# A hybrid decoder layer on one core: the output projection in seven block products instead of eight

## The chip, the cores and the metric

The kernel runs on one core of a Trainium2 chip. The metric is the device time of one execution in microseconds (us); the value given for a kernel is the median of its runs. The core has a matrix engine (TensorE, PE in the profile), three elementwise engines (VectorE = DVE, ScalarE = ACT, GpSimd = POOL), and SyncE (SP), which here only starts transfers. Each engine works through its own queue strictly in order and waits at the head of it for whatever its next instruction needs.

## The reference

One layer for x of 512 tokens by 1024 channels, all in float32. Two token mixers (a retention with 8 heads and a gated delta rule with 8 heads) are merged by sigmoid gates; their merged output is multiplied by `w_o` (1024 x 1024) and added to x; a gated MLP with a short causal convolution follows. What matters here:

```python
merged = jax.nn.sigmoid(gate_r) * y_ret + jax.nn.sigmoid(gate_d) * y_dn
h = h + merged @ w_o[l]

u2 = rmsnorm(h, g_ffn[l])
up = causal_dwconv(u2 @ w_up[l], ffn_conv_w[l]) + ffn_conv_b[l]
a, b = jnp.split(up, 2, axis=-1)
h = h + (jax.nn.silu(a) * b) @ w_down[l]
```

## The kernel before

**Products.** A float32 operand is split into two fp32r parts, hi (a cast) and lo (the value minus hi), and a product is made of three matmuls: hi by hi, lo by hi, hi by lo. All matmuls are issued from line 175 and all transposes from line 179, so groups are told apart by tile: `pvt`, `pqk`, `pm`, `psc` belong to the two mixers, `pz` and `py` to the gates and branch projections, `po` is the output projection, `pa` and `pb` the up projection, `pd` the down projection. Every elementwise operation goes through one helper, line 160.

**Weights.** They come as blocks of 128 x 1024 numbers: SP loads a block into one of 4 `wraw` tiles (lines 242 and 244), ACT casts it to `whi`, DVE subtracts to get `wlo` (`weights()`; 4 tiles of each). A block that has been used frees its tiles for the block four places later.

**Seven products.** The four matrices of the gates and branches (`matrix(s)`, s = 0 to 3, tile `py`) and the down projection are multiplied as 2 x 2 blocks with seven products of blocks instead of eight (table `PRODUCTS`). Four of the seven need sums of weight blocks (`SUMS`), which POOL makes beforehand in memory by transfers that copy or accumulate, 1 MB each (`presum`, line 265). They are paced: `presums(which, parts, (start, end, n))` sends a piece when the order's clock passes its time, and each piece is preceded by a one-column copy on ACT (`tick`) and one on POOL that waits for it (`tock`).

**The output projection before.** `dense_r` makes it plainly: 8 weight blocks, 192 matmuls of 128 x 512 on all four token tiles. Its operand is made by `m_out`: four transposes on PE (`pmt`), a cast on ACT (`mh`), a subtraction on DVE (`ml`). `o_done` adds each result to `h1`, which is loaded from x (line 1262) after the last branch matrix; then come the sum of squares (`junk`, `ssq`), its root (`rs` on DVE, `rr` on POOL), the scaling (`hs`, two instructions a token tile), four transposes (`pt`), and the split into `u2hi` (ACT) and `u2lo` (DVE), 8 each a token tile. The first three up-projection blocks are made in two halves of 256 tokens (`dense_c_halves`), so that they can start when two of the four token tiles are ready.

**The order.** The program is written in the order in which a small planner, `Order`, takes its steps: `spawn` adds a step with a delay, `poll` lets steps run that are due by the planner's clock, `hold` runs them until an operand exists. The order on PE, DVE, ACT and POOL stays as written. So a change of one time in the planner moves rows on all engines.

Of the kernel before, what the change touches and what calls it, by code (L numbers as in the profile page):

```python
# [18 lines left out]
P = 128  # L19
T = 512  # L20
# [36 lines left out]
DOWN = 4  # L57
INNER = (HK, HK, HK, HK, NK)
# [5 lines left out]
def quarter_blocks(s):  # L64
    n = INNER[s]
    return [("q", s, name, i, min(2, n - 2 * i)) for name, _ in PRODUCTS for i in range((n + 1) // 2)]


def weight_blocks():
# [14 lines left out]
    for o in (0, 512):  # L84
        b += [("r", "w_o", 2 * i, o) for i in range(4)]
# [96 lines left out]
def body(nc, tc, ctx, io):  # L182
# [66 lines left out]
    sums = {(s, n): dram.tile([P, 512 * INNER[s] + 64], F32, name=f"{n}_{s}") for s in range(5) for n, _, _ in SUMS}  # L249
# [84 lines left out]
    def dense_c_halves(x, names, ready_half, first=None):  # L334

        ws, pss = [], [PS(n) for n in names]
        for hf in range(2):
            c = ck(hf, 256)
            for i, ps in enumerate(pss):
                if hf == 0:  # L340
                    ws.append(take("c"))
# [6 lines left out]
                if hf:  # L348
                    used()
# [33 lines left out]
    def product(p, opnd, nk, accs, tail=0):  # L383
# [7 lines left out]
        def block(i, t, c, ps, first):  # L391
# [136 lines left out]
    def fetch_more():  # L528
        free[0] += RAWB - 2
# [171 lines left out]
    spawn(presums(range(3), 1, (90.0, 325.0, 24)), 30.0)  # L701
# [475 lines left out]
    spawn(presums((3,), 1, (order.clock + 5.0, order.clock + 75.0, 8)))  # L1177
    mh, ml = {}, {}
# [3 lines left out]
    def m_tile(k, t):  # L1182
        i = k // HK
        if (t, i) not in ml:
            return None
        return mh[t, i][:, ck(k % HK)], ml[t, i][:, ck(k % HK)]

    def m_out(t, i, r):
# [3 lines left out]
        hi, lo = S(f"mh{t}{i}", F32R), S(f"ml{t}{i}", F32R)  # L1192
        yield from split(hi, lo, pt)
        mh[t, i], ml[t, i] = hi, lo
# [22 lines left out]
    def matrix(s, opnd):  # L1217
# [17 lines left out]
        def prod(p, accs, tail=0):  # L1235
            now[0] = len(PRODUCTS) * s + p
            product(p, opnd, HK, accs, tail)
# [21 lines left out]
    h1 = [[S(f"h1_{t}{i}") for i in range(2)] for t in range(NT)]  # L1259
    for t in range(NT):  # L1260
        for i in range(2):
            sp.dma_start(h1[t][i], xv[t, :, ck(i, T)])
# [4 lines left out]
    def o_done(i):  # L1267
        def done(t, _, ps):
            vec.tensor_tensor(h1[t][i], ps, h1[t][i], ALU.add)
            yield  # L1270
            junk = S("junk")
            half_ssq(ssqs[t], i, h1[t][i], junk)
            if i == 0:
                return
            yield
            rr = s4("rr", 1)
            yield from row_scale(ssqs[t], rr)
            yield
            for i2 in range(2):
                xs = S("hs")  # L1280
                vec.tensor_scalar(xs, h1[t][i2], rr, None, ALU.mult)
                spawn(u2_out(t, i2, xs), 0.6 * (i2 + 1))
        return done
# [14 lines left out]
    for i in range(2):  # L1298
        dense_r([PS("po") for _ in range(NT)], m_tile, done=o_done(i), groups=((0, 1), (2, 3)) if i else ((2, 3), (0, 1)))
# [56 lines left out]
    pss = dense_c_halves(u2, ("pa", "pb", "pa"), u2_half)  # L1356
# [66 lines left out]
    def down(p, accs, tail=0):  # L1423
        at[0] = p
        product(p, parts, NK, accs, tail)
# [101 lines left out]
```

## Time and profile before

| | us |
|---|---|
| median of 3 runs | 1020.42 |
| the runs | 1019.91 to 1023.36 |
| the profiled execution's own time | 1017.77 |
| its span, first to last instruction | 1016.1 |
| PE busy | 992.6 |
| DVE busy | 716.9 |
| ACT busy | 514.9 |
| POOL busy | 154.7 |

The profile comes from one execution, so durations and places are read against 1017.77 us, and a difference found there is then carried to the median. Times in rows count from the start of the span. A row of the timeline gives start, duration, engine, line, operation, output and inputs, count, and in brackets how long the engine stood idle before it and what released it. Matmuls overlap: a row says 0.39 us for a matmul, but in a full pipe the next starts 0.227 us later. Likewise the next instruction of DVE can start a little before the row of the one ahead ends.

### The profile page before, as it was taken

What the parts mean: (1) busy time and instruction counts of PE and PEld (TensorE: products, weight loads), DVE (VectorE), ACT (ScalarE), POOL (GpSimd) and SP (SyncE); (2) the same over time, 40 slices, a digit from 0 to 9 for tenths busy, and PEclk for the clock granted to TensorE, in tenths of its full rate; (3) what the DMA queues carried; (4) which work ended last, traced back from release to release, by engine and by line L of the source; (5) the groups of instructions that cost most, each with busy time, mean ns of one, the idle gap of its engine ahead of it and who ended that gap; (6) DMA issues with size and microseconds to landing.
All of it is one profiled execution on the core that took longest, in us unless ns stands there. A gap on an engine that the chain in (4) does not pass through costs nothing.

```text
span 1016.1 us, 14340 instructions
## 1 busy us (share of the span) xinstructions
PE 992.6 (98%) x5265; PEld 827.2 (81%) x5265; DVE 716.9 (71%) x1344; ACT 514.9 (51%) x1092; POOL 154.7 (15%) x204
## 2 busy tenths in 40 slices
PE   7999899999999999999999998999999999999997
PEld 7888788787788887878888886898888888888886
DVE  4867699456777797647688984576555666778785
ACT  4699312276445423547676652454344343356664
POOL 3021311123222211211110000211121121000001
PEclk8999999999999999999999999999999999999999
DMA  7253659736846853027998656556589988336663
GB/s 242 84 152 107 186 167 209 197 121 159 173 162 177 196 130 109 27 77 270 281 302 244 189 193 212 178 192 212 191 170 197 199 178 189 99 120 190 204 191 120
DMA packets 78550, 177.75 MB, mean 175 GB/s; under 512 B 22864, under 2 KB 31376, under 8 KB 78480
## 3 DMA queue, kind: packets, MB, share of 16 engines
q1 hardware_dynamic: 54160, 120.22, 36.1%
q0 software_dynamic: 24320, 56.63, 25.5%
q8 instruction: 41, 0.67, 0.3%
q14 instruction: 29, 0.24, 0.1%
HBM read 173.64 MB, written 59.80 MB: 230 GB/s over the span
## 4 chain that ended last, share of the span: by engine, by line
PE 76%; DVE 13%; DMA 4%; issue 2%; ACT 2%; POOL 1%; SPq 1%; POOLq 0%; DVEq 0%; ACTq 0%
PE py L175 14%; PE pb L175 12%; PE pa L175 12%; PE pd L175 10%; PE po L175 4%; PE pq L175 4%; PE pk L175 3%; PE pz L175 3%; PE pv L175 3%; DVE wlo L160 3%; DVE xtmp L160 3%; PE psc L175 2%; DVE xx L160 2%; PE pm L175 1%; PE pr L175 1%
## 5 line engine op out<-in xcount | busy, mean ns | idle before, releaser
L160 ACT CAST whi<-wraw 128x1024 fp32r<-128x1024 f32 x206 | 213.4, 1036 | 153.0 <-PE py L175 41.4
L160 DVE TENSOR_TENSOR wlo<-wraw,whi 128x1024 fp32r<-128x1024 f32 x206 | 248.4, 1206 | 45.9 <-ACT whi L160 45.4
L160 POOL TENSOR_SCALAR tock<-tick 128x1 f32<-128x1 f32 x64 | 21.0, 328 | 466.0 <-ACT tick L160 466.0
L160 DVE SCALAR_TENSOR_TENSOR acc<-pb,prm,acc 128x511 f32<-128x511 f32 (+1 forms) x44 | 33.0, 749 | 57.2 <-ACT acc L160 56.4
L175 PE MATMUL pa<-u2lo,whi 128*128 128x512 f32 (+1 forms) x192 | 71.5, 372 | 0.1
L175 PE MATMUL pa<-u2hi,whi 128*128 128x512 f32 (+1 forms) x192 | 71.4, 372 | 0.0
L175 PE MATMUL pa<-u2hi,wlo 128*128 128x512 f32 (+1 forms) x192 | 71.4, 372 | 0.0
L175 PE MATMUL pb<-u2hi,whi 128*128 128x512 f32 (+1 forms) x184 | 70.0, 380 | 0.0
L175 PE MATMUL pb<-u2lo,whi 128*128 128x512 f32 (+1 forms) x184 | 70.0, 380 | 0.0
L175 PE MATMUL pb<-u2hi,wlo 128*128 128x512 f32 (+1 forms) x184 | 70.0, 380 | 0.0
L175 PE MATMUL py<-whi,oh 128*128 128x512 f32 x160 | 62.7, 392 | 0.0
L175 PE MATMUL py<-wlo,oh 128*128 128x512 f32 x160 | 62.4, 390 | 0.0
L175 PE MATMUL py<-whi,ol 128*128 128x512 f32 x160 | 62.3, 390 | 0.0
L175 PE MATMUL pd<-whi,T 128*128 128x512 f32 (+1 forms) x198 | 55.4, 366 | 0.0
L175 PE MATMUL pr<-whi,uhi 128*128 128x512 f32 x128 | 53.0, 414 | 0.0
L175 PE MATMUL pz<-uhi,whi 128*128 128x512 f32 x128 | 52.3, 409 | 0.0
L175 PE MATMUL pr<-whi,ulo 128*128 128x512 f32 x128 | 50.6, 395 | 0.0
L175 PE MATMUL pr<-wlo,uhi 128*128 128x512 f32 x128 | 50.5, 394 | 0.0
L175 PE MATMUL pz<-uhi,wlo 128*128 128x512 f32 x128 | 50.0, 391 | 0.0
L175 PE MATMUL pz<-ulo,whi 128*128 128x512 f32 x128 | 50.0, 390 | 0.0
L160 DVE SCALAR_TENSOR_TENSOR acc<-pa,prm,acc 128x511 f32<-128x511 f32 (+1 forms) x44 | 33.0, 749 | 19.0 <-ACT acc L160 18.2
L175 PEld LDWEIGHTS pa<-u2lo,whi 128*128 128x128 f32 x192 | 36.2, 188 | 6.6 <-DVE u2lo L160 0.3
(313 smaller groups left out, 2447.6 us busy)
## 6 DMA issues: line engine op xcount, KB each, us to landing
wraw<-w SPq DMA_DIRECT2D x108, 512.0 KB, 4.3
wraw<-s SPq DMA_DIRECT2D x52, 512.0 KB, 4.4
s<-wm POOLq DMA_DIRECT2D x24, 1024.0 KB, 6.9
s<-wd POOLq DMA_DIRECT2D x24, 704.0 KB, 5.5
wraw<-wm SPq DMA_DIRECT2D x24, 512.0 KB, 5.8
s<-s POOLq DMA_DIRECT2D x8, 1024.0 KB, 10.9
wraw<-wd SPq DMA_DIRECT2D x15, 512.0 KB, 3.6
s<-s POOLq DMA_DIRECT2D x8, 704.0 KB, 8.9
```

The lines of the kernel that those rows point to most:

```text
L160: return f(out, *args, **kw)
L175: self.engine.matmul(out, lhsT, rhs, start=start, stop=stop, **kw)
```

## The change

The output projection becomes an instance of the seven products, as matrix `OUT` = 4 (the down projection becomes 5). It is 168 matmuls on 14 weight blocks instead of 192 on 8. The products come in the order 0, 3, 2, 5, 4, 1, 6, that is with the operands B11, T1, T2, B22, T3, B21, T4 of the merged activations. `m_out` now copies the transposed tile to memory (`mr`, ACT), DVE makes the combinations T1 to T4 (`mt1` to `mt4`), and each operand is split (cast on ACT, subtraction on DVE, tiles `mB11`, `mT1` and so on). `o_into` adds 14 results to `h1` instead of 8. The token tiles 2 and 3 are complete before 0 and 1, so the first up-projection halves are made in the order second, first.

Times that go with it: the weight sums of matrices 0 to 2 start at 110 of the planner's clock instead of 90 (end and count as before); those of matrix 3 start within the stage of the z gates instead of after it; those of `w_o`, 8 pieces, run from the end of matrix 0; the 8 loads of `h1` move from behind matrix 3 to ahead of it. `fetch_more` waits for a condition; the rows on SP at that place read as before.

```diff
-DOWN = 4
-INNER = (HK, HK, HK, HK, NK)
+OUT, DOWN = 4, 5
+INNER = (HK, HK, HK, HK, HK, NK)
+OUT_ORDER = (0, 3, 2, 5, 4, 1, 6)
...
-    spawn(presums(range(3), 1, (90.0, 325.0, 24)), 30.0)
+    spawn(presums(range(3), 1, (110.0, 325.0, 24)), 30.0)
...
         if x == "d":
             spawn(u_raw(), 8.0)
+            spawn(presums((3,), 1, (order.clock + 8.0, order.clock + 70.0, 8)))
...
-    spawn(presums((3,), 1, (order.clock + 5.0, order.clock + 75.0, 8)))
...
+        m = o_raw[name, half] = S(f"mr{t}{i}")
+        act.copy(m, pt)
+        yield
+        if name in ("B11", "B21"):
+            spawn(o_split(name, half, m))
+        if name == "B12":
+            t1 = S("mt1")
+            vec.tensor_tensor(t1, o_raw["B11", half], m, ALU.subtract)
+            spawn(o_split("T1", half, t1), 0.2)
+            yield
+            t3 = S("mt3")
+            vec.tensor_tensor(t3, o_raw["B22", half], m, ALU.subtract)
+            t2 = o_raw["T2", half] = S("mt2")
+            vec.scalar_tensor_tensor(t2, t3, -1.0, o_raw["B11", half], ALU.mult, ALU.subtract)
+            spawn(o_split("T2", half, t2), 0.2)
+            yield 1.5
+            spawn(o_split("B22", half, o_raw["B22", half]), 0.2)
+            spawn(o_split("T3", half, t3), 1.8)
+        elif name == "B21":
+            yield 1.5
+            t4 = S("mt4")
+            vec.scalar_tensor_tensor(t4, o_raw["T2", half], -1.0, m, ALU.mult, ALU.subtract)
+            spawn(o_split("T4", half, t4), 0.2)
...
+    spawn(presums((OUT,), 1, (order.clock, order.clock + 75.0, 8)))
+    h1 = [[None] * 2 for _ in range(NT)]
     for s, opnd in ((1, u_opnd), (2, d_opnd), (3, r_opnd)):
+        if s == 3:
+            for t in range(NT):
+                for i in range(2):
+                    h1[t][i] = S(f"h1_{t}{i}")
+                    sp.dma_start(h1[t][i], xv[t, :, ck(i, T)])
         matrix(s, opnd)
...
-    for i in range(2):
-        dense_r([PS("po") for _ in range(NT)], m_tile, done=o_done(i), groups=((0, 1), (2, 3)) if i else ((2, 3), (0, 1)))
+    A, E, C = ([PS("po") for _ in range(2)] for _ in range(3))
+    product(0, o_get, HK, [[(full, A[t], True, o_into(t, 0, A[t], ALU.add))] for t in range(2)])
+    product(3, o_get, HK, [[(full, E[t], True, o_into(2 + t, 1, E[t], ALU.subtract))] for t in range(2)])
+    product(2, o_get, HK, [[(full, A[t], False, o_into(2 + t, 0, A[t], ALU.add))] for t in range(2)])
+    product(5, o_get, HK, [[(full, E[t], False, o_into(2 + t, 0, E[t], ALU.add, True))] for t in range(2)])
+    product(4, o_get, HK, [[(full, A[t], False, o_into(2 + t, 1, A[t], ALU.subtract, True))] for t in range(2)])
+    product(1, o_get, HK, [[(full, C[t], True, o_into(t, 0, C[t], ALU.add, True))] for t in range(2)])
+    product(6, o_get, HK, [[(full, A[t], False, o_into(t, 1, A[t], ALU.subtract, True))] for t in range(2)], tail=2)
...
-    pss = dense_c_halves(u2, ("pa", "pb", "pa"), u2_half)
+    pss = dense_c_halves(u2, ("pa", "pb", "pa"), u2_half, order_=(1, 0))
```

Where the change moves rows, three places matter for the prediction. (In these rows the lines of the changed kernel are one higher, since it has one line more at its head.)

POOL, before, in the first heads of the delta rule. `ssk` and `ssqq` are sums of squares of the keys and queries of a head, `rk` and `rq` their roots, `gb` the head's decay tile, `s` a weight sum in memory:

```order
L160 TENSOR_TENSOR rq<-ssqq,mhalf 128x4
L160 TENSOR_SCALAR tock<-tick 128x1
L265 DMA s_0_77<-wm 128x4x512
L160 TENSOR_TENSOR rk<-ssk,mhalf 128x4
L160 AFFINE_SELECT gb_967<-gb_967 128x512
L160 MEMSET xx 64x1024
```

POOL at the same place now:

```order
L161 TENSOR_TENSOR rq<-ssqq,mhalf 128x4
L161 TENSOR_TENSOR rk<-ssk,mhalf 128x4
L161 AFFINE_SELECT gb_971<-gb_971 128x512
L161 MEMSET xx 64x1024
L161 MEMSET xx 64x32
L161 TENSOR_TENSOR rq<-ssqq,mhalf 128x4
L161 TENSOR_SCALAR tock<-tick 128x1
L266 DMA s_0_77<-wm 128x4x512
```

The first `tock` and its transfer stood ahead of the fourth head's `rk`; they now stand behind everything that this head asks of POOL.

DVE, before, at the beginning of the output projection (numbers tell tiles apart; `ml20` is the lo part of token tile 2, first half of the channels):

```order
L160 TENSOR_TENSOR wlo_6260<-wraw_6134,whi_6247 128x1024
L160 TENSOR_TENSOR ml20_6253<-pmt_6197,mh20_6252 128x512
L160 TENSOR_TENSOR ml30_6263<-pmt_6255,mh30_6262 128x512
L160 TENSOR_TENSOR ml01_6276<-pmt_6266,mh01_6275 128x512
L160 TENSOR_TENSOR ml11_6301<-pmt_6290,mh11_6300 128x512
L160 TENSOR_TENSOR h1_20_6206<-po_6240,h1_20_6206 128x512
```

DVE now, from the second half's T3 to the lo part of T2 (`mT2_6395`) that product 2 reads; further on, nine rows later, stands the lo part of B22 (`mB22_6471`) that product 5 reads:

```order
L161 TENSOR_TENSOR mt3_6384<-mr31_6216,mr30_6314 128x512
L161 SCALAR_TENSOR_TENSOR mt2_6386<-mt3_6384,mr10_6096 128x512
L161 TENSOR_TENSOR h1_00_5878<-h1_00_5878,po_6295 128x512
L161 TENSOR_TENSOR h1_10_5882<-h1_10_5882,po_6296 128x512
L161 TENSOR_TENSOR mT4_6382<-mt4_6376,mT4_6381 128x512
L161 SCALAR_TENSOR_TENSOR mt4_6416<-mt2_6386,mr11_6378 128x512
L161 TENSOR_TENSOR wlo_6418<-wraw_6253,whi_6391 128x1024
L161 TENSOR_TENSOR mT2_6395<-mt2_6386,mT2_6394 128x512
```

Before, DVE had four subtractions there; now combinations, splits and additions follow one another.

DVE, before, where the first two token tiles are scaled, in the middle of the output projection:

```order
L160 SCALAR_TENSOR_TENSOR rs_6525<-ssq1_6235 128x1
L160 TENSOR_SCALAR hs_6550<-h1_10_6204,rr_6524 128x512
L160 TENSOR_SCALAR hs_6552<-h1_11_6205,rr_6524 128x512
L160 TENSOR_TENSOR wlo_6558<-wraw_6386,whi_6535 128x1024
L160 SCALAR_TENSOR_TENSOR u2lo0_6226<-pt_6527,prm_99,u2hi0_6218 128x128
```

DVE now, at its end. `h1_11` is the last addition, which needs the last matmul of product 6:

```order
L161 TENSOR_TENSOR h1_11_5884<-h1_11_5884,po_6296 128x512
L161 TENSOR_TENSOR wlo_6688<-wraw_6629,whi_6672 128x1024
L161 SCALAR_TENSOR_TENSOR rs_6693<-ssq1_6294 128x1
L161 TENSOR_TENSOR wlo_6695<-wraw_6653,whi_6685 128x1024
L161 SCALAR_TENSOR_TENSOR junk_6699,ssq1_6291<-h1_01_5880 128x512
L161 TENSOR_SCALAR hs_6702<-h1_20_5886,rr_6679 128x512
L161 TENSOR_SCALAR hs_6704<-h1_21_5888,rr_6679 128x512
L161 SCALAR_TENSOR_TENSOR junk_6706,ssq1_6292<-h1_11_5884 128x512
L161 TENSOR_SCALAR hs_6725<-h1_30_5890,rr_6692 128x512
L161 TENSOR_SCALAR hs_6727<-h1_31_5892,rr_6692 128x512
L161 SCALAR_TENSOR_TENSOR u2lo0_6283<-pt_6708,prm_103,u2hi0_6275 128x128
```

The scaling of the first two finished token tiles, which stood in the middle of the projection with po matmuls after it, now stands behind its last addition; on PE the 16 transposes `pt` of these tiles stand behind the last po matmul.

More of the change, by code (lines that the diff above doesn't have):

```diff
@@ L65, in quarter_blocks @@
     n = INNER[s]
-    return [("q", s, name, i, min(2, n - 2 * i)) for name, _ in PRODUCTS for i in range((n + 1) // 2)]
+    order = OUT_ORDER if s == OUT else range(len(PRODUCTS))
+    return [("q", s, PRODUCTS[p][0], i, min(2, n - 2 * i)) for p in order for i in range((n + 1) // 2)]
 def weight_blocks():
@@ L246, in fetch @@
             raws[i] = raw
-    sums = {(s, n): dram.tile([P, 512 * INNER[s] + 64], F32, name=f"{n}_{s}") for s in range(5) for n, _, _ in SUMS}
+    sums = {(s, n): dram.tile([P, 512 * INNER[s] + 64], F32, name=f"{n}_{s}") for s in range(DOWN + 1) for n, _, _ in SUMS}
     def quarter(s, name):
@@ L416, in product, with by_half, get @@
                 spawn(then, 0.1 if tail else 0.1 + 0.7 * t)
+    def by_half(x):
+        def get(name, k, t):
+            return (name, k) in x and tuple(a[:, ck(t)] for a in x[name, k])
+        return get
     def halves(a):
@@ L528, in fetch_more @@
     def fetch_more():
+        while "G" not in have:
+            yield 0.5
         free[0] += RAWB - 2
@@ L1176, in body, with o_get, o_split @@
     spawn(all_operands())
-    spawn(presums((3,), 1, (order.clock + 5.0, order.clock + 75.0, 8)))
-    mh, ml = {}, {}
     gates = [{}, {}]
     merged = {}
[L1182 to L1186, printed above, removed]
+    o_raw, o_opnd = {}, {}
+    def o_get(name, k, t):
+        return (name, t) in o_opnd and tuple(a[:, ck(k)] for a in o_opnd[name, t])
+    def o_split(name, t, src):
+        hi, lo = S(f"m{name}", F32R), S(f"m{name}", F32R)
+        yield from split(hi, lo, src)
+        o_opnd[name, t] = hi, lo
     def m_out(t, i, r):
@@ L1191, in m_out @@
         yield
-        hi, lo = S(f"mh{t}{i}", F32R), S(f"ml{t}{i}", F32R)
-        yield from split(hi, lo, pt)
-        mh[t, i], ml[t, i] = hi, lo
+        name, half = f"B{i + 1}{t // 2 + 1}", t % 2
+        m = o_raw[name, half] = S(f"mr{t}{i}")
[21 more added lines that the diff above has]
+            spawn(o_split("T4", half, t4), 0.2)
     def gate_end(s, t, i, r, ps):
@@ L1236, in prod @@
             now[0] = len(PRODUCTS) * s + p
-            product(p, opnd, HK, accs, tail)
+            product(p, by_half(opnd), HK, accs, tail)
         A, C = ([PS("py") for _ in range(2)] for _ in range(2))
@@ L1265, in body, with o_into @@
     ssqs = [s4("ssq1", 2) for _ in range(NT)]
[L1267 to L1283, printed above, removed]
+    def o_into(t, i, ps, op, last=False):
+        vec.tensor_tensor(h1[t][i], h1[t][i], ps, op)
+        yield
+        if not last:
+            return
+        junk = S("junk")
+        half_ssq(ssqs[t], i, h1[t][i], junk)
+        if i == 0:
+            return
+        yield
+        rr = s4("rr", 1)
+        yield from row_scale(ssqs[t], rr)
+        yield
+        for i2 in range(2):
+            xs = S("hs")
+            vec.tensor_scalar(xs, h1[t][i2], rr, None, ALU.mult)
+            spawn(u2_out(t, i2, xs), 0.6 * (i2 + 1))
     u2_ready = set()
@@ L1424, in down @@
         at[0] = p
-        product(p, parts, NK, accs, tail)
+        product(p, by_half(parts), NK, accs, tail)
     A, C, E = ([PS("pd") for _ in range(2)] for _ in range(3))
```

20 lines of the change are left out of this document (7 added, 13 removed).

## The prediction

> **What bounds the kernel now.** I read the page first: the busy times and the chain that ended last.
>
> ```profile
> PE 992.6 (98%) x5265; PEld 827.2 (81%) x5265; DVE 716.9 (71%) x1344; ACT 514.9 (51%) x1092; POOL 154.7 (15%) x204
> PE 76%; DVE 13%; DMA 4%; issue 2%; ACT 2%; POOL 1%; SPq 1%; POOLq 0%; DVEq 0%; ACTq 0%
> ```
>
> PE is the bound: 23.5 of its 1016.1 us are idle. A change therefore gains by fewer matmuls or by one of PE's few waits, and loses by a new wait. So I read next the view of PE's waits, summed by what ended them.
>
> ```profile
> PE po L175 <- DVE ml L160: 3.0, 1, 3.0
> PE pvt L179 <- ACT v L160: 2.9, 1, 2.9
> PE pm L175 <- DMA tt<-x_dram: 2.5, 3, 1.4
> PE psc L175 <- DVE Sn L160: 1.7, 2, 1.2
> ```
>
> Three of the four lie where the change moves something: at the start of po, at the fourth head's `pvt`, and at `pm`, fed through memory. The windows say how full DVE is around the output projection:
>
> ```profile
> 600.00:615.00 15.00, 11.44 (x60) 9.13 (x58) 14.83 (x21) 6.92 (x10) 0.96 (x2) 1.00 0.73 245
> 615.00:662.00 47.00, 46.95 (x210) 38.79 (x211) 21.68 (x43) 15.40 (x38) 7.63 (x14) 0.96 0.52 175
> ```
>
> The columns are the window, its length, then busy time and count of PE, weight loads, DVE, ACT, POOL. DVE is full before 615 (14.83 of 15) and less than half full behind it (21.68 of 47). The first window's lateness is the 3.0 us wait of po.
>
> **The front, line 110 for 90.** The chain of waits around the fourth head, then DVE's timeline there:
>
> ```profile
> 104.82 0.09 ACT tick L160
> ...
> 105.00 0.23 POOL tock L160
> 105.23 0.91 POOL s L265
> ...
> 106.15 1.08 POOL rk L160
> ...
> 111.17 0.64 ACT v L160
> ...
> 111.85 0.66 PE pvt L179 x4
> ```
>
> ```profile
> 101.52 0.17 DVE L160 TENSOR_SCALAR ssk<-ssk 128x4 f32<-128x4 f32 x1
> 107.25 0.16 DVE L160 TENSOR_TENSOR c<-beta,rk 128x4 f32<-128x4 f32 x1 [5.57 <-POOL rk L160]
> ```
>
> POOL stood at `tock` until ACT reached its `tick` at 104.82, behind other work; `rk` was queued behind, though its input was there at 101.7; behind DVE's wait for `rk` stood everything that makes `v`, for which PE waited. In the new order `rk` is ahead of `tock`. It can run from 101.7 to 102.8, so `c` starts near 102.9 instead of 107.25, 4.3 us earlier, and `v` near 111.17 - 4.3 = 106.9. PE was at `pvt` at 111.85 - 2.93 = 108.9. The wait goes: **-2.9**. What is late next is PE itself, so no more than that. The bound below is that `v` waits for something else on DVE for a part of it (0), and above the 2.9.
>
> Presums start later and so stand at other places against the transfers through memory:
>
> ```profile
> 171.81 5.81 DMA x_dram<-xx
> 180.85 7.06 DMA tt<-x_dram
> 187.96 1.27 PE pm L175 x22
> ```
>
> ```profile
> 112.00:116.00 4.00, 4.00 (x25) 3.51 (x25) 2.79 (x6) 1.85 (x6) 2.67 (x3) 1.00 0.57 149
> 188.60:192.00 3.40, 3.40 (x13) 2.25 (x11) 0.81 (x3) 0.00 (x0) 0.00 (x0) 0.50 0.95 335
> 615.30:618.70 3.40, 3.40 (x9) 2.63 (x9) 0.89 (x2) 0.00 (x0) 0.00 (x0) 0.50 1.05 416
> ```
>
> PE waits up to 1.4 us for `tt` (the row of waits; the one that ends at 187.96), and behind it the granted clock, the last column but two of the windows, is 0.50 for 3.4 us: 1.7 us lost. Weight sums moved beside both transfers, and they still do in the new order, two pieces earlier in their sequence. Between nothing and the whole (1.4 + 1.7 = 3.1) I take **-0.5**, nearer to nothing, since as many pieces now go in less time. From 200 to 340 us many rows change places without anything being added; I put 0 there, with 1.5 either way, about the `psc` row above (1.7 in all).
>
> **The z stage.** The 8 sums of matrix 3 now stand there, between the heads' roots on POOL:
>
> ```profile
> 433.02 1.01 POOL L160 TENSOR_TENSOR ro<-mso,mhalf 128x4 f32<-128x4 f32 x1 [0.88 <-DVE mso L160]
> 442.96 1.02 POOL L160 TENSOR_TENSOR ro<-mso,mhalf 128x4 f32<-128x4 f32 x1 [7.69 <-DVE mso L160]
> 460.98 0.85 POOL L265 DMA_DIRECT2D s<-wm  x1
> ```
>
> A `tock` and its issue hold POOL about 1.1 us, and longer if the tick is late. A head's `ro` behind it is late by that, and PE has `pz` matmuls to do meanwhile; if these were used up, two heads late would cost 2.2. I take +0.1, from 0 to 2.2.
>
> **The branch products.** They run 133 us without a wait:
>
> ```profile
> 455.00:588.00 133.00, 133.00 (x589) 110.20 (x588) 110.00 (x153) 91.42 (x137) 12.91 (x16) 1.00 0.81 251
> 606.63 3.87 SPq L1262 DMA_DIRECT2D h<-x  x8
> wraw<-wm SPq DMA_DIRECT2D x24, 512.0 KB, 5.8
> ```
>
> The sums of `w_o` take over the place on the transfer engines from those of matrix 3, which ran there before: nothing. The 8 loads of `h1` now stand on SP between weight blocks, and hold the blocks behind them by up to 3.87 us. A block is used for 12 matmuls, 2.72 us, so a wraw tile comes round in 10.9 us; cast, subtraction (2.2) and landing (5.8) take 8, which leaves 2.9. So at most 1 us is late, and PE's 4 split blocks cover that: +0.2, from 0 to 3.
>
> **The output projection.** Its timeline on PE, and DVE's prices, from DVE's and ACT's timelines:
>
> ```profile
> 609.30 1.03 PE L179 MATMUL pmt<-cst,res 128*128 128x128 f32 x8
> 611.64 0.40 PE L175 MATMUL po<-wlo,mh 128*128 128x512 f32 x1
> 615.05 0.63 PE L175 MATMUL po<-whi,ml 128*128 128x512 f32 x1 [3.01 <-DVE ml L160]
> 662.14 0.28 PE L175 MATMUL pa<-u2hi,whi 128*128 128x256 f32 x1
> ```
>
> ```profile
> 613.18 1.22 DVE L160 TENSOR_TENSOR wlo<-wraw,whi 128x1024 fp32r<-128x1024 f32 x1
> 614.32 1.88 DVE L160 TENSOR_TENSOR ml<-pmt,mh 128x512 fp32r<-128x512 f32 x3
> 651.52 1.19 DVE L160 TENSOR_SCALAR hs<-h,rr 128x512 f32<-128x512 f32 x2 [0.47 <-POOL rr L160]
> 653.32 2.16 ACT L160 ACTIVATE u2hi<-pt,prm 128x128 fp32r<-128x128 f32 x8
> 655.42 4.22 DVE L160 SCALAR_TENSOR_TENSOR u2lo<-pt,prm,u2hi 128x128 fp32r<-128x128 f32 x16
> 639.85 12.48 PE po L175 x55
> ```
>
> From the end of py to the first pa it takes 662.14 - 609.30 = 52.84 us. 55 matmuls in 12.48 make 0.227 each: 192 are 43.6; eight groups of four transposes at 0.44 make 3.5; the waits 3.6; and behind the wait matmuls start 0.43 apart, not 0.227, until 618.8, about 1.9. Without any wait the new stage would be 168 x 0.227 + 3.5 = 41.6: 11.2 us less. That is what the change offers.
>
> Against it stands DVE. It gets 6 more `wlo` (1.14 apart), 6 more splits, 8 combinations and 6 more additions (0.6 apart each): 6.8 + 12 = 19 us more, in a shorter time. I walked the new DVE queue with these spacings, ACT's casts at 1 (a block) and 0.5 (a tile) between, and 0.1 from engine to engine. (PE ahead of 609.3 as in the rows.) Product 0 ends at 616.2, product 3 at 621.6. The second half of T2: its last `mr` is there at 613.4, but DVE has T1 and the first halves of T2, T4 and B21 with three `wlo` in its queue ahead of it, starts `mt3_6384` at 621.4, and has two additions, two rows of T4 and a `wlo` between that and `mT2_6395` (626.3, done at 627.0). PE arrives at 623.0, waits 0.6 for the cast, does one matmul, and waits another 3.3. Product 2 ends at 630.9. The lo of B22, second half, is done at 633.5, PE waits 1.1; product 5 ends at 637.4, product 4 at 642.8, 1 at 648.3, 6 at 653.7. So the waits are 5.0 where they were 3.6, and po ends 8.2 us earlier than at 661.9.
>
> Then the tail. DVE does the last addition 0.6, `wlo` 1.14, `rs` 0.13, `wlo` 1.14, `ssq` 0.69 (3.7), two `hs` 0.8, `ssq` 0.69, two `hs` 0.8 (6.0), and 9 `u2lo` at 0.26 with an `rs` between (8.5). The second matmul of pa needs the ninth `u2lo`: it starts 8.8 behind the last po matmul, at 662.5. Transposes and `u2hi` run beside. What hid this chain before were po matmuls on the other token tiles; nothing hides it now. That gives back all of the 8.2.
>
> The clock. In the windows quoted at the front it is 1.00 behind the 2.9 us wait at 109, and 0.50 for 3.4 us behind the shorter wait at 187 and behind that of 3.0 at 612. So a wait of 3 us may cost another 1.7 or not. The tail holds PE nearly idle for 8.8 us, so I count it there: +1.7. At product 2 it may come too, but product 5 would then wait 1.1 less; 0.6 at half a chance is +0.3. The 1.7 of before is in its 662.14 already.
>
> [...]
>
> Against the row at 662.14 the second matmul of pa (662.26) comes at 662.5: +0.3. With 1.7 and 0.3 the stage is **+2.3**: it costs what it was to bring. Behind that, halves and up projection have the same work as before. The ends are -1.5 (no low clock at either place, and DVE 2 us ahead of my walk) and +4 (the clock low at both, and DVE 1.5 behind it).
>
> **Sum.** -2.9 - 0.5 + 0.1 + 0.2 + 2.3 = -0.8 against 1017.77, which is 2.65 below the median of the runs (1020.42). Carried to the median: **1019.6 us**. A difference under 0.3%, about 3.1 us, can't be told from none.
>
> **Rivals.**
>
> *The 11.2 us are had in part or whole.* If DVE's backlog at T2 and in the tail is hidden (the combinations done while py still runs, the `hs` reached before the last addition ends), the stage falls towards 41.6: at most -11.2 - 3.1, 1006; with half of it, 1012. For it: ACT and POOL have room, and the order follows the operands. Against: DVE is full already in 600 to 615, and the tail's rows stand behind an addition that can't come earlier. 0.20: faster.
>
> *Slower, by late weight blocks.* The `h1` loads and the blocks behind them compete; if a block lands more than 2.9 us late (decided by the landing of the blocks behind the loads: above 8.7 instead of 5.8), PE waits up to 3.9 and loses 1.7 by the clock: +5.6 - 0.8, 1025. The row of landings speaks for only a part of that. 0.15: slower.
>
> *The front's gain is swallowed.* If PE, earlier at `pm`, only waits there longer for `tt`, -2.9 becomes 0: +2.1, 1022.5. Against: that chain starts from the same head and comes earlier too. 0.10, of which 0.03 slower.
>
> **Chances.** The forecast has 0.55. The ends of its terms won't all fall together; with two at an end on either side (`pm` -2.6 and the reordering -1.5, or the stage +1.7 and the loads +1) it goes from -4.9 to +1.9, so 0.10 of it lies past -3.1 and the rest is no change. Faster 0.10 + 0.20 = 0.30, same 0.45 + 0.07 = 0.52, slower 0.15 + 0.03 = 0.18. For 8 in 10 the range takes in the half of the 11.2 and the swallowed gain with a part of the late blocks: 1012 to 1024.
>
> **What would show it.** In the new profile: no wait of `pvt` for `v`; a wait of po for `mT2` near 3, one for `mB22` near 1; a stretch of 8 to 9 us between the last po and the second pa with only transposes on PE, and 0.24 apart behind it for 128x256. DVE over nine tenths busy from 610 to 645. I am wrong if po to pa closes without that stretch, or if py shows waits for `whi` behind the `h1` loads.

## The result and the profile after

| | before | after |
|---|---|---|
| median of 5 runs, us | 1019.91 | 1029.89 |
| the runs | 1016.4 to 1023.36 | 1029.71 to 1030.32 |
| ratio (95% interval) | | 1.01 (1.0074 to 1.0126) |
| span of the profiled execution | 1016.1 | 1028.0 |

The changed kernel is 10 us slower, with 24 matmuls fewer; the forecast was 1019.6, in a range that ended at 1024. The page of the changed kernel, its busy line and its chain:

```profile
PE 993.4 (97%) x5241; PEld 826.0 (80%) x5241; DVE 733.9 (71%) x1370; ACT 528.7 (51%) x1120; POOL 168.9 (16%) x220
PE 76%; DVE 14%; DMA 4%; issue 3%; ACT 2%; POOL 1%; SPq 0%; POOLq 0%; DVEq 0%
```

PE is busy longer with fewer instructions (993.4 against 992.6). 24 matmuls at 0.227 are 5.4 us, so the others took some 6 us more: at a lower clock (mean granted 0.985, before 0.993). PE's waits in the changed kernel, summed by what ended them (total, times, longest):

```profile
PE pm L176 <- DMA tt<-x_dram: 6.2, 3, 4.3
PE pt L180 <- DVE hs L161: 4.2, 1, 4.2
PE py L176 <- DVE ol L161: 2.8, 2, 2.0
...
PE psc L176 <- DVE R L161: 2.0, 2, 1.7
...
PE po L176 <- DVE mT L161: 1.6, 1, 1.6
PE po L176 <- ACT mT L161: 1.5, 1, 1.5
PE py L176 <- ACT oh L161: 1.4, 1, 1.4
...
PE po L176 <- DVE mB L161: 0.7, 1, 0.7
PE pa L176 <- DVE u2lo L161: 0.7, 1, 0.7
```

The wait of `pvt` is gone and that of po is spread, as forecast. New are 6.2 for `tt` (2.5 before; 5.2 and 1.2 of them in the z stage), 4.2 for `ol` and `oh` in the branch products, which had no wait, and 4.2 for `hs`. The windows show the stages, two at the times of the windows before (the first two) and the places of the new waits; the granted clock is the last column but two:

```profile
112.00:116.00 4.00, 4.00 (x20) 3.30 (x19) 2.46 (x7) 1.05 (x1) 0.00 (x0) 1.00 0.49 142
188.60:192.00 3.40, 3.40 (x33) 2.72 (x33) 1.88 (x4) 0.97 (x4) 0.21 (x1) 1.00 0.94 343
386.70:393.50 6.80, 4.57 (x25) 3.49 (x25) 1.27 (x5) 0.73 (x2) 0.00 (x0) 0.50 0.45 119
455.00:588.00 133.00, 132.61 (x586) 109.46 (x584) 100.98 (x140) 85.06 (x128) 13.21 (x17) 1.00 0.89 268
588.00:600.00 12.00, 8.16 (x27) 6.13 (x28) 11.44 (x15) 8.66 (x14) 0.00 (x0) 0.72 0.54 178
600.00:615.00 15.00, 15.00 (x71) 12.39 (x71) 12.84 (x18) 8.26 (x11) 0.00 (x0) 1.00 0.64 199
615.00:662.00 47.00, 43.26 (x196) 34.78 (x195) 42.81 (x60) 24.92 (x41) 7.62 (x13) 1.00 0.71 238
662.00:682.00 20.00, 15.13 (x88) 13.94 (x87) 11.95 (x35) 8.65 (x29) 4.33 (x7) 0.74 0.44 150
```

Full clock now at 188.6 (0.50 before). The trip through memory for which PE waited there now comes 10 us earlier: PE waits 1.01 at 178.0, and the window from 16 to 386 has a clock of 1.00. Half clock stands at three new places, and DVE is busy 42.81 of 47 in the output projection, where it had 21.68.

To put the 11.9 us of the spans in place I read in the timelines where each tile's matmuls begin and end. The profiles of all kernels below are in the same table, in us. The stages are those of one execution each, the ratio is that of all runs of a kernel; where a kernel was profiled twice, its z stages differ by up to 1.6 and its stages from the end of py by up to 2.8.

| kernel | first pz | z stage | branch products (py) | end of py to end of pa | ratio to before (95%) |
|---|---|---|---|---|---|
| before | 335.3 | 119.5 | 154.0 | 289.8 | |
| after | 328.6 | 128.1 | 161.8 | 292.0 | 1.0100 (1.0074 to 1.0126) |
| e1 | 328.3 | 126.3 | 157.0 | 289.8 | 1.0013 (0.9991 to 1.0034) |
| e2 | 327.8 | 124.8 | 164.0 | 292.1 | 1.0073 (1.0049 to 1.0098) |
| e3 | 328.4 | 122.9 | 157.1 | 292.3 | 0.9987 (0.9964 to 1.0009) |
| e4 | 328.4 | 121.2 | 154.0 | 289.8 | 0.9945 (0.9925 to 0.9964) |
| e5 | 328.0 | 123.2 | 155.4 | 291.7 | 0.9990 (0.9966 to 1.0014) |
| e6 | 328.4 | 121.5 | 155.7 | 286.0 | 0.9944 (0.9924 to 0.9963) |
| e7 | 327.6 | 121.1 | 155.0 | 295.7 | 1.0024 (0.9998 to 1.0049) |
| e8 (before again) | 335.5 | 119.2 | 154.0 | 289.8 | |
| e9 | 329.2 | 127.7 | 156.7 | 291.0 | 1.0029 (1.0009 to 1.0048) |
| e10 | 328.2 | 122.9 | 155.1 | 285.5 | 0.9903 (0.9873 to 0.9933) |
| e11 | 333.2 | 126.7 | 162.6 | 290.0 | 1.0098 (1.0060 to 1.0135) |
| e12 (after again) | 328.5 | 127.1 | 162.4 | 291.8 | 1.0115 (1.0091 to 1.0139) |
| e13 | 339.3 | 119.9 | 156.1 | 282.4 | 0.9968 (0.9945 to 0.9991) |
| e14 (e10 again) | 328.7 | 121.3 | 156.2 | 282.7 | 0.9913 (0.9880 to 0.9947) |
| e15 (e4 again) | 328.4 | 120.6 | 154.0 | 289.8 | 0.9951 (0.9936 to 0.9967) |

From before to after: -6.7 up to the first pz, +8.6 in the z stage, +7.8 in the branch products, +2.2 from the end of py to the end of pa, nothing behind it. So two stages, which the forecast had at +0.1 and +0.2, cost 16.4 us.

**The z stage.** POOL, SP and PE of the changed kernel around the second of the two trips through memory (`x_dram`, then `tt`), one view of the timeline each (start, duration, engine, line, operation, and in brackets the idle time ahead and its releaser):

```profile
381.38 1.81 POOL L161 TENSOR_SCALAR tock<-tick 128x1 f32<-128x1 f32 x1 [27.17 <-ACT tick L161]
383.14 0.82 POOL L266 DMA_DIRECT2D s<-wm  x1
...
428.54 1.32 POOL L266 DMA_DIRECT2D s<-wm  x1
429.37 1.59 POOL L161 TENSOR_TENSOR ro<-mso,mhalf 128x4 f32<-128x4 f32 x1
```

```profile
379.71 0.48 SPq L829 DMA_DIRECT2D x_dram<-xx  x1
383.29 9.44 SPq L832 DMA_DIRECT2D tt<-x_dram  x16
```

```profile
387.99 0.31 PE L176 MATMUL pm<-tt,A 32*32 32x32 f32 x2 [4.29 <-DMA tt<-x_dram]
389.24 0.63 PE L176 MATMUL pm<-tt,A 32*32 32x32 f32 x14 [0.94 <-DMA tt<-x_dram]
...
433.14 0.49 PE L176 MATMUL psc<-R,tt 128*128 128x128 f32 x2 [1.71 <-DVE R L161]
```

A weight sum of 1 MB is issued at 383.14, just ahead of the loads of `tt`, for which PE waits 4.29 and 0.94. Then PE works at half clock until 393.5 (4.57 busy, half of it lost: 2.3). Later another sum is issued between a `tock` and a `ro`, and PE waits 1.71 for `R`. These make 9.2 of the stage, against 1.2 for `tt` and 0.3 for `R` before. The 16 loads of `tt` took 1.6, 3.1 and 4.9 us from issue to landing (least, median, most); in the kernel before, where the last sums had been issued at 344.5 and 356.6 and landed within 11.5 us, 1.6, 1.8 and 3.2 (issued from 388.78 to 397.34).

**The branch products.** SP's timeline and its waits for transfers from 570 to 590 (total, times, longest), then ACT's and PE's timelines:

```profile
571.28 5.97 SPq L1295 DMA_DIRECT2D h<-x  x8
579.09 13.90 SPq L243 DMA_DIRECT2D wraw<-s  x6
```

```profile
SPq L243 <- DMA h<-x: 5.1, 4, 2.8
...
SPq L1295 <- DMA wraw<-s: 2.0, 1, 2.0
```

```profile
587.41 1.04 ACT L161 CAST whi<-wraw 128x1024 fp32r<-128x1024 f32 x1 [7.39 <-PE py L176]
```

```profile
589.03 0.51 PE L176 MATMUL py<-whi,oh 128*128 128x512 f32 x1 [1.42 <-ACT oh L161]
590.37 0.50 PE L176 MATMUL py<-whi,ol 128*128 128x512 f32 x1 [0.83 <-DVE ol L161]
...
593.30 0.79 PE L176 MATMUL py<-whi,ol 128*128 128x512 f32 x1 [1.97 <-DVE ol L161]
```

Between 571.28 and 579.09 SP issues no weight block. Of these 7.8 us the issue of the eight loads itself takes 3.9, as at its old place. For the rest SP stands and waits for landings: 2.0 ahead of the eighth load, 1.8 ahead of the block (L243), and 2.8 more ahead of the block after that. What it waits for is each time the transfer eight places ahead in its own order: the load issued at 571.28 lands 7.7 later, at 579.0, and the block goes out at 579.09. What sets the eight was not tried. That block lands 8.2 after its issue, at 587.3. Until then ACT stands 7.39 at its cast; `oh`, whose input is there, is queued behind that cast, and `ol` on DVE behind both. PE's first wait stands at the first matmul of that block, so the split blocks that it held were used up. PE waits 4.2 in all, and 588 to 600 has a clock of 0.72 (8.16 busy, 2.3 lost). The bracket of ACT's row names PE, whose matmul ended at the same moment; the landing at 587.3, 0.1 ahead of the cast, speaks for the block, and the experiments test it.

**The output projection's end.** DVE and PE of the changed kernel:

```profile
663.35 0.69 DVE L161 TENSOR_TENSOR h<-h,po 128x512 f32<-128x512 f32 x1 [1.64 <-PE po L176]
...
666.91 0.88 DVE L161 TENSOR_SCALAR hs<-h,rr 128x512 f32<-128x512 f32 x2
...
668.31 0.88 DVE L161 TENSOR_SCALAR hs<-h,rr 128x512 f32<-128x512 f32 x2
```

```profile
662.93 0.39 PE L176 MATMUL po<-wlo,mT 128*128 128x512 f32 x1
667.53 3.65 PE L180 MATMUL pt<-cst,hs 128*128 128x128 f32 x16 [4.22 <-DVE hs L161]
671.14 0.58 PE L176 MATMUL pa<-u2hi,whi 128*128 128x256 f32 x1
672.38 0.58 PE L176 MATMUL pa<-u2lo,whi 128*128 128x256 f32 x1 [0.65 <-DVE u2lo L161]
```

This is the forecast tail: the second pa starts 9.2 us after the last po has been fed (672.38 - 663.16), with only transposes between.

### The profile page after: what moved, and what is told of

It reads as the page before. It is cut to its first block, busy times and chain, and to the rows that moved or that the text cites. A ratio compares the mean times of both kernels' runs of the same rounds, so it can differ in the third digit from the quotient of the medians.

```text
span 1028.0 us, 14392 instructions
## 1 busy us (share of the span) xinstructions
PE 993.4 (97%) x5241; PEld 826.0 (80%) x5241; DVE 733.9 (71%) x1370; ACT 528.7 (51%) x1120; POOL 168.9 (16%) x220
## 4 chain that ended last, share of the span: by engine, by line
PE 76%; DVE 14%; DMA 4%; issue 3%; ACT 2%; POOL 1%; SPq 0%; POOLq 0%; DVEq 0%
PE py L176 14%; PE pa L176 12%; PE pb L176 12%; PE pd L176 10%; DVE wlo L161 4%; PE pq L176 4%; PE pk L176 3%; PE pz L176 3%; PE pv L176 3%; PE psc L176 3%; PE pr L176 3%; DVE xtmp L161 3%; PE po L176 2%; DVE xx L161 2%; PE pm L176 2%
## 5 line engine op out<-in xcount | busy, mean ns | idle before, releaser
L161 ACT CAST whi<-wraw 128x1024 fp32r<-128x1024 f32 x212 | 219.6, 1036 | 151.6 <-PE py L176 46.3
L161 DVE TENSOR_TENSOR wlo<-wraw,whi 128x1024 fp32r<-128x1024 f32 x212 | 254.7, 1203 | 52.9 <-ACT whi L161 52.5
L161 POOL TENSOR_SCALAR tock<-tick 128x1 f32<-128x1 f32 x72 | 27.8, 387 | 533.9 <-ACT tick L161 524.9
```

Of the source, the lines that this page charges most:

```text
L161: return f(out, *args, **kw)
```

## The experiments

The theory: three separate places pay, each for rows that were moved into somebody's way: the sums of matrix 3 in the z stage, the loads of `h1` in SP's queue in the branch products, and `hs` behind the late additions on DVE at the end of po. The rivals: the loads hurt by the bytes that they move and not by their place on SP; the seven products can't gain here at all; and the gain of the front is swallowed by later waits, whatever the rest does. Each run is the changed kernel with the edit shown, unless said otherwise. All keep the computation whole.

**e1: `h1` loaded where it was.**

```diff
-        if s == 3:
-            for t in range(NT):
...
-                    sp.dma_start(h1[t][i], xv[t, :, ck(i, T)])
         matrix(s, opnd)
...
     spawn(presums((DOWN,), 4, (order.clock, order.clock + 230.0, 32)))
+    for t in range(NT):
...
+            sp.dma_start(h1[t][i], xv[t, :, ck(i, T)])
```

> The changed kernel with the 8 loads of h1 put back behind matrix 3; nothing else differs. Theory L (the loads hold up the weight blocks of matrix 3 on SP): the 7.4 us in which ACT waits for a block near 580, PE's waits for oh and ol (4.2 in all) and the low clock behind them go, and the branch products from first to last py matmul take about 143 us instead of 151; the kernel gains 5 to 8 us, unless the loads now hold up blocks of w_o, where a wait of 2 to 5 would stand at the start of po. Rival S (the sums of w_o, which run beside matrices 1 to 3, hold the blocks up by traffic): the wait near 580 stays, and the time is within 2 us of the changed kernel.

Measured: 1021.32 (before on this chip 1020.71). py takes 157.0, 4.8 less; the wait for `oh` is gone, 2.0 for `ol` is left. So the loads' place is the larger part of py's 7.8. The z stage is 1.8 shorter as well, though every engine's rows stand there in the same order as in the changed kernel, and the stage of po 2.2, though its waits are the same (4.2 for `hs`, 0.65 for `u2lo`): there the clock is low for 3.4 us instead of 10.2, on which the last section has more. This edit alone, then, did not bring the whole ratio.

**e2: the sums of matrix 3 where they were.**

```diff
-            spawn(presums((3,), 1, (order.clock + 8.0, order.clock + 70.0, 8)))
...
     spawn(all_operands())
+    spawn(presums((3,), 1, (order.clock + 5.0, order.clock + 75.0, 8)))
```

> The changed kernel with the weight sums of matrix 3 put back behind the z stage (5 to 75 of the clock after it); nothing else differs. Theory Z (a sum's transfer beside the loads of tt, and its issue ahead of ro on POOL, made the z stage longer): the 4.3 us wait of pm for tt and the low clock behind it go, psc waits 1.2 less, and the stage from first to last pz matmul takes about 120 us instead of 128; that is 6 to 9 us up to there, a part of which may be lost in the branch products, where the sums of two matrices then run side by side. Rival R (the rows that change places shift the chain that makes xx, whatever the sums do): pm still waits 3 us or more for tt.

Measured: 1025.95. The z stage falls by 3.3 to 124.8, not to 120, and the wait of psc for `R` of 1.7 is gone, but 4.0 for `tt` stays, the sign that rival R named. The order of rows is not the reason, though: in e2, e3 and e4 the rows stand in the same order on every engine up to 20 us ahead of the first py, and PE waits 4.0, 2.7 and 2.5 for `tt`, with half clock for 6.8, 3.4 and 0 us in the stage. So the same rows scatter between executions. On average the four kernels with the changed kernel's sums in the stage (after, e1, e9, e12) take 127.3, the four without (e2, e3, e4, e15) 122.4, and the two profiles of before 119.4: the sums cost some 5, and 3 come with 110 alone. py grows to 164.0, where the sums of matrix 3 and of `w_o` now stand together with the loads; this run doesn't separate them.

**e3: both back, the sums of 3 and of `w_o` as one list of 16 behind the z stage.**

```diff
-            spawn(presums((3,), 1, (order.clock + 8.0, order.clock + 70.0, 8)))
...
+    spawn(presums((3, OUT), 1, (order.clock + 5.0, order.clock + 140.0, 16)))
...
-    spawn(presums((OUT,), 1, (order.clock, order.clock + 75.0, 8)))
```

(and the loads as in e1)

> The changed kernel with both put back, the h1 loads behind matrix 3 and the sums of matrix 3 behind the z stage, and the sums of w_o queued behind those (16 pieces over 135 of the clock). What is left of the change is the front and the output projection. If L and Z hold and nothing else is at work: the front's gain (5 to 7 us up to the first pz) stays, z stage and branch products are as before, and the output projection costs 2 to 3: about 1015 to 1017 on the scale on which the kernel before has 1020. By S or R it stays at 1024 or more.

Measured: 1019.7, no difference from before, and some 3 us above what was expected. z 122.9, py 157.1, still 3.4 and 3.1 above before. po's stage is 292.3, as in the changed kernel: putting back what was moved returns more than half of what the other two stages lost, and this one has gained nothing.

**e4: the kernel before, with 110 alone.** Eight products, nothing else changed.

```diff
-    spawn(presums(range(3), 1, (90.0, 325.0, 24)), 30.0)
+    spawn(presums(range(3), 1, (110.0, 325.0, 24)), 30.0)
```

> The kernel before with one number changed: the weight sums of matrices 0 to 2 start at 110 instead of 90. Theory F (the front's gain comes from taking the first tick and tock out of the fourth head's chain): pvt doesn't wait for v, the first pz matmul comes 4 to 6 us earlier, and the kernel gains 3 to 6 us. Rival N (the front's gain in the changed kernel is scatter between executions at the start, 1.6 us by the first pr matmul, and luck of the reordering): within 2 us of the kernel before.

Measured: 1013.2, a ratio of 0.9945 (0.9925 to 0.9964): the front brings 5.6 us by itself, more than the 3.4 of the forecast. The first pz comes 6.9 earlier, and the z stage gives 1.7 back: PE, earlier at `pm`, waits 2.5 for `tt` there (1.2 before) without any sum near.

**e5: e1, with the sums of 3 in two pieces and those of `w_o` behind the z stage.**

```diff
-            spawn(presums((3,), 1, (order.clock + 8.0, order.clock + 70.0, 8)))
+            spawn(presums((3,), 1, (order.clock + 22.0, order.clock + 46.0, 3), (order.clock + 70.0, order.clock + 110.0, 5)))
...
+    spawn(presums((OUT,), 1, (order.clock + 30.0, order.clock + 92.0, 8)))
...
-    spawn(presums((OUT,), 1, (order.clock, order.clock + 75.0, 8)))
```

(and the loads as in e1)

> The changed kernel with the h1 loads behind matrix 3 (as in e1) and the weight sums at chosen times: those of matrix 3 in two groups in and behind the z stage, clear of the loads of tt and of the ro on POOL (3 pieces at 22 to 46 of the clock from the second half of the stage, 5 at 70 to 110), those of w_o 30 to 92 behind the stage, done before matrix 3. Theory: with e1 at 1021.3, psc no longer waits 1.7 for R, pm waits 2 to 3 as in the kernel before with 110, and the waits of py for ol (2.0 in e1, late blocks beside the sums of w_o) go: py takes 154, as before; 4 to 6 us faster than e1, 1015 to 1017. Rival (matrix 3's operands are late for another reason, rows that changed places on DVE): py keeps its 157 and the run is above 1018.

Measured: 1018.28, a little above what was expected. z 123.2, with 0.3 for `R` instead of 2.0, py 155.4 with 0.7 for `ol`. The five kernels that have the sums at these times (e5, e6, e7, e10, e14) average 122.0 in z, as much as those with no sum of matrix 3 there: the times of the sums, not the fact that they are made in the z stage, cost there.

**e6: e5, with `hs` ahead of the late additions.** The planner is told of an earlier due time in `o_into`, so that the scaling of token tiles 2 and 3 is written ahead of the additions of products 1 and 6.

```diff
         vec.tensor_tensor(h1[t][i], h1[t][i], ps, op)
-        yield
+        yield -4.0
```

(likewise at the yields between `ssq`, `rs` and `hs`)

> e5 with one thing more: the four steps from the addition of a finished token tile to its scaling (sum of squares, rs, rr, hs) are put into the order 4 us of the planner's clock earlier each, so that on DVE the hs of token tiles 2 and 3 stand ahead of the additions of products 1 and 6. No work is added or taken out. Theory T (the tail behind product 6 is DVE's order: what stood between the last addition and hs): PE's wait of 4.2 for hs and of 0.7 for u2lo and the low clock of 7 to 10 us behind them go, and from the end of py to the end of pa it takes 8 to 11 us less than the 292 of e3: 6 to 10 us faster than e5. Rival D (DVE simply has too much to do, the order only shifts where PE waits): the waits move into products 1 and 6, and the gain is under 3 us.

Measured: 1014.56, 0.9944 of before. The wait for `hs` falls from 4.2 to 0.7, po's stage from 291.7 to 286.0: the row order at the end of po held 5.7 us, wait and low clock together. Against e1 and e11, where the clock behind the same wait was low for 3.4 us only, it is 3.8 and 4.0. Expected were 8 to 11 less than in e3, and 6.3 were measured; new waits of 1.2 and 0.8 for `u2hi` and `u2lo` of the second halves take a part back. So the stage can gain: 3.8 against before.

**e7: e6, with DVE relieved.** The second halves' sums of squares go to ACT, `mt1` and `mt3` to POOL.

```diff
-            vec.tensor_tensor(t1, o_raw["B11", half], m, ALU.subtract)
+            pool.tensor_tensor(t1, o_raw["B11", half], m, ALU.subtract)
...
-        half_ssq(ssqs[t], i, h1[t][i], junk)
+        act.activation(junk, h1[t][i], AF.Square, scale=1.0 / 32.0, accum_out=ssqs[t][:, i:i + 1])
```

> e6 with work taken off DVE in the output projection: the second half's sum of squares goes to ACT (4 instructions of 0.69) and the combinations T1 and T3 go to POOL (4 of 0.6). Theory (po's waits at T2 and B22, 1.5 and 1.6 and 0.7 in the changed kernel, are DVE's backlog): they fall to under 1.5 in sum, and the run is 2 to 3 us faster than e6. Rival (POOL's slower additions and its queue of sums bring the operands no earlier): within 1 us of e6 or slower.

Measured: 1022.1, worse than e6. po's own operand waits fall from 3.7 to 2.0, but the timeline of PE has this:

```profile
641.09 1.94 PE L180 MATMUL pt<-cst,hs 128*128 128x128 f32 x8 [4.44 <-DVE hs L161]
...
659.79 1.70 PE L180 MATMUL pt<-cst,hs 128*128 128x128 f32 x8 [2.27 <-DVE hs L161]
```

`hs` and its transposes now stand too early in the order, and PE stands at the transposes 8.7 us in all (two waits of 1.2 and 0.8 are not shown). Whether the relief is right and only the due time wrong, e10 takes apart.

**e8: the kernel before, once more**, for the spread of its profile.

> The kernel before, unchanged, for a second profile: how much the beginning differs between executions. If the 1.6 to 2.6 us by which all kernels with 110 reach the first pr matmul earlier are scatter of the first loads, this profile shows the first pr between 99 and 101 too; if they come from the change, it shows 101.8 again. pvt waits 2.9 in either case.

Measured: a span of 1015.9 and the same stages within 0.3 us. The first pr matmul comes at 100.1, as in the kernels with 110 and not at 101.8: the earlier start is scatter. `pvt` waits 2.94, but here the clock is low behind it, as the last section tells, so the first pz comes at 335.5 all the same.

**e9: `h1` loaded at the changed kernel's place, but issued by POOL.** The same bytes at about the same time, and SP's queue free.

```diff
-                    sp.dma_start(h1[t][i], xv[t, :, ck(i, T)])
+                    nc.gpsimd.dma_start(h1[t][i], xv[t, :, ck(i, T)])
```

> The changed kernel with the 8 loads of h1 issued by POOL instead of SP, at the same point of the order (behind the last sum of w_o); the bytes are the same, but no weight block stands behind them in a queue. Theory Q (the blocks were late because they stood behind the loads on SP): the 7.4 us hole in ACT's casts near 580 goes, py takes about 157 as in e1, and the run is 6 to 8 us faster than the changed kernel. Theory B (2 MB beside the blocks and a sum are too much for the transfers, whoever issues them): the hole stays with 4 us or more, py takes 161 or more.

Measured: 1022.76; py 156.7, 5.1 less than in the changed kernel. The loads take longer to land (15.4 in the median, 10.6 in the changed kernel), but SP no longer waits for them, and ACT's hole at the same cast is 3.04 instead of 7.39, now with the block named:

```profile
567.27 21.16 SPq L243 DMA_DIRECT2D wraw<-s  x8
```

```profile
582.85 1.05 ACT L161 CAST whi<-wraw 128x1024 fp32r<-128x1024 f32 x1 [3.04 <-DMA wraw<-s]
```

So it was the place on SP and not the bytes: the 2.7 that is left against 154.0 is no more than the 3.0 of e1, where the loads are not there at all. What holds these 3 us was not separated. In the changed kernel's trace the issue of the loads takes SP 3.9 us, and SP also stood 2.0 and 1.8 us for landings before the block went out. With the loads on POOL's queue py is 5.1 shorter, so here more than the 3.9 of the issue was saved.

**e10: e7 with the due times moved back** (`yield -1.0` for `yield -4.0`).

> e7 with the four steps only 1 us earlier each instead of 4: with less work on DVE the planner had put hs, and PE's transposes that read it, too far forward, so that PE stood 8.7 us at pt. Theory: that wait goes (under 1.5 in sum), the smaller waits of po from e7 (1.9 instead of 3.7) stay, and the second halves of the up projection find their operand: 2 to 4 us faster than e6, 1010.5 to 1012.5. Rival (POOL's combinations cost more than DVE's backlog): no faster than e6.

Measured: 1009.83, 0.9903 (0.9873 to 0.9933). po's stage is 285.5, 10.2 less than in e7 with nothing changed but the due times; `pt` still waits 2.6 for `hs` (1.0 in e14). This version beats both kernels.

**e11: the changed kernel with 90 again.**

> The changed kernel with the weight sums of matrices 0 to 2 starting at 90 again. Theory F: pvt waits 2.9 for v again, the first pz comes near 335 instead of 328.6, and the run takes 5 to 8 us more than the changed kernel: 1035 to 1038. Rival: PE's earlier arrival in the z stage was lost there at tt anyway, and the run is within 3 us of the changed kernel.

Measured: 1030.45, 1.0098 of before. `pvt` waits its 2.9 again and the first pz is 4.6 later, but the profile ends only 2.0 later: the z stage is 1.4 shorter, by PE's shorter wait for `tt`, and the clock behind po is low for 3.4 us only. The 5 to 8 us that were expected are not there; in the changed kernel the front's gain can't be seen in the time. With four runs the interval is wide enough to hide some 3 us of it.

**e12 to e15, on one chip**, to settle whether the front's gain and that of the seven products reach the end. e12 is the changed kernel again, e14 is e10 again, e13 is e14 with 90 in place of 110, e15 is e4 again.

> The changed kernel once more, beside the runs below. Both theories expect about 1.01 of the kernel before, some 10 us slower (1.0074 to 1.0126 was measured). If it comes out under 1.004, the earlier figure was the chip and not the change.

> The fastest kernel so far (raw v loads apart, sums of matrix 3 in two pieces, hs ahead of the late additions, relief of VectorE in the output projection) with 90 again in place of 110. Theory A, the front's gain arrives wherever the z stage doesn't give it back: 5 to 7 us over the same kernel with 110, about 1015 to 1017. Theory B, most of the front's gain is swallowed by whatever the output projection waits for: 0 to 2 us over it.

(The raw v loads that it names are not in its edit; what stands apart there are the loads of `h1`, as in e1.)

> The fastest kernel so far, unchanged. About 0.990 of the kernel before (0.9873 to 0.9933 was measured), some 1010 us.

> The kernel before with 110 in place of 90, and eight products. About 0.9945 of the kernel before, some 1013 us. If the seven products bring a gain of their own once their sums and loads stand in nobody's way, the run above lies 3 to 5 us under this one; if they bring none, the two are within 2 us.

Measured against 1017.67 for before on this chip: 1029.03, 1014.85, 1009.34 and 1013.27. e13 lies 5.5 us over e14, as the front's gain had been found by itself in e4. e14 lies 3.9 under e15; the intervals of the two ratios overlap a little (0.9880 to 0.9947 and 0.9936 to 0.9967), but the ratios of e10 and e4 lay as far apart (0.0042, here 0.0038), and the stages say where it comes from: -7.1 in po's stage (282.7 for 289.8; the same kernel had 285.5 as e10), +2.2 in py, +0.7 in z. The windows of e14 over po and the start of pa, and PE's timeline at the seam:

```profile
606.40:652.10 45.70, 42.76 (x198) 34.01 (x197) 42.14 (x68) 30.05 (x62) 15.89 (x18) 1.00 0.80 277
652.10:672.00 19.90, 19.90 (x164) 19.45 (x163) 13.66 (x31) 10.68 (x30) 4.16 (x6) 1.00 0.65 216
```

```profile
652.08 0.39 PE L176 MATMUL po<-wlo,mT 128*128 128x512 f32 x1
652.31 0.28 PE L176 MATMUL pa<-u2hi,whi 128*128 128x256 f32 x1
```

DVE is nine tenths busy as in the changed kernel, but pa follows po without a gap and the clock stays full.

## Why the prediction was wrong

**The front: right in place, too small.** The `pvt` wait is gone in every kernel with 110, and in the kernel before with 110 alone the first pz comes 6.9 earlier, for a forecast of -2.9 - 0.5. 1.6 of the changed kernel's 6.7 stand ahead of the first pr matmul (100.2 for 101.8), and e8 has them without the change (100.1). The step that failed is "Between nothing and the whole (1.4 + 1.7 = 3.1) I take **-0.5**". The wait for `tt` stayed (1.0 for 1.4), but the half clock behind it went, 1.7: all four profiles with 90 (before, e8, e11, e13) have it, none of the 13 with 110. And in two of the four, e8 and e13, the `pvt` wait is followed by half clock too, for which the forecast had nothing. The third rival saw the gain's fate in the changed kernel in part: e11 shows none of it there. But that is due to what stands behind it, since e4, e13 and e14 show it in the time.

**The z stage: wrong, +8.6 for "+0.1, from 0 to 2.2".** The step "PE has `pz` matmuls to do meanwhile" held for the roots only in part (1.71 at `R`), and I priced the sums by the roots on POOL alone. The larger cost is on the transfers: `x_dram` and `tt` also run in this stage, and a sum of 1 MB went out just ahead of the loads that PE waits for, which then took 3.1 us in the median to land instead of 1.8. An earlier PE waits longer there anyhow (2.5 in e4, 1.2 before). I had looked at that very wait at 188 and forgot it at 388. e5 and its kin show that other times for the same sums take some 5 of it back; about 1 of the 8.6 is scatter, since the kernels with the same rows there have 126.3 to 128.1.

**The branch products: wrong, +7.8 for "+0.2, from 0 to 3".** The failed step is "So at most 1 us is late, and PE's 4 split blocks cover that". It took 3.87 for the time that the loads hold SP. Their issue did take 3.9, but SP also had to wait 2.0 and 1.8 for landings, and the next block left 7.8 after the first load and landed 0.1 ahead of a cast that came 7.4 late; PE's split blocks were used up by then. And the step counted only what PE holds in blocks, not that `oh` and `ol` stand behind the late block's cast in ACT's and DVE's queues; the sign that I had named, waits of py behind the loads, came for these and not for `whi`. The rival "Slower, by late weight blocks" had the wait and gave 5.6 for it, but tied it to a landing of the blocks above 8.7. The landings of the blocks would not have shown it, those of the loads do: in the changed kernel (565 to 600) the rows read

```profile
wraw<-s SPq DMA_DIRECT2D x8, 512.0 KB, 6.2
h<-x SPq DMA_DIRECT2D x8, 256.0 KB, 10.6
```

so the blocks were not slow in landing but late in issue, behind loads that were slow in landing. "The sums of `w_o` take over the place ... nothing" is not refuted; what they cost by themselves was not tried.

**The output projection: right, +2.2 for +2.3.** The last po is fed 44.2 after the end of py (forecast 44.4), the second pa 9.2 after that (forecast 8.8). Inside, T2 waited 1.45 and 1.59 instead of 0.6 and 3.3, B22 0.7 instead of 1.1. The clock cost about what was set down (0.50 from 672.4, where the second pa starts, to 676.8: 2.2 us lost, for 1.7 and 0.3), though it came in the tail alone, and longer (10.2 us in all). That the sum agrees to 0.1 is luck: with the same waits the stage is 289.8 in e1 and 292.1 in e2, by the clock alone. That the 11.2 us can be had in part, the first rival, is true of e10 and e14 (4.3 and 7.1), not of this change.

**The sum.** -6.7 + 8.6 + 7.8 + 2.2 = 11.9, the difference of the spans. Two terms of 0.1 and 0.2 carried ends of 2.2 and 3; both measured at about 8: in both, a wait for the landing of a transfer was put at nothing, so the bounds were wrong, and the range with them.

## What to carry to other kernels

Whoever moves paced transfers prices every queue that they are moved past, and asks above all whether a store and a load that PE waits for lie there; a transfer that lands late also counts for what stands behind it in the queue that issued it (SP stood 2.0, 1.8 and 2.8 us here). A late block delays not just its own matmuls but everything written behind its cast on the in-order engines (here ACT stood 7.39 us at that cast, and PE then 4.2 for the `oh` and `ol` behind it). And a stage with fewer matmuls gains only when the last rows of the engine that feeds the next stage stand ahead of the rows that nobody waits for: that alone was 3.8 to 5.7 us here, by the clock that went with it.

## What the runs showed of the hardware

The same wait does not always bring the same clock. The `pvt` wait is 2.93 in the profile of before and 2.94 in e8; behind the first the clock was 1.00 (112 to 116, shown with the prediction), behind the second it was this:

```profile
110.00:113.60 3.60, 3.51 (x15) 3.32 (x16) 2.47 (x6) 2.19 (x7) 2.02 (x3) 0.53 0.55 155
```

Nor does the length of a wait decide: the wait of 1.36 ahead of `pm` at 188.0 in before is followed by half clock from 188.6 to 192.0, the one of 1.53 at 177.7 in e15 is not:

```profile
176.00:186.00 10.00, 8.40 (x101) 6.13 (x101) 4.88 (x13) 1.52 (x6) 1.50 (x2) 1.00 0.89 140
```

And the low clock does not always last as long: in e1 it was low for 3.4 us behind the 4.22 us wait for `hs`, in the changed kernel for 10.2 from the last 0.9 of the same wait on; the waits being the same, this is what makes the 2.2 us between their stages. In e13 a wait of 1.78 that ended at 187.7 was followed by a low clock until 201.5:

```profile
186.00:202.00 16.00, 14.30 (x108) 10.91 (x109) 5.00 (x13) 2.70 (x7) 0.00 (x0) 0.57 0.71 230
```

Waits as short as 1.36 (before), 1.71 (e11, ended at 185.80) and 1.78 (e13) had half clock behind them, and the clock stayed low for 3.4 us in e1, 10.2 in the changed kernel and 13.7 in e13. Why it falls behind one wait and not behind another, and what sets how long it stays low, was not settled.
